# Mixer A of a two-layer hybrid trunk put into a fixed order: projections two heads ahead, both maps' logits side by side, two of mixer B's convolution inputs drawn into A

## The chip, the cores and the metric

The kernel runs on one core of one Trainium2 chip, as one launch. The metric is the device time of an execution in microseconds; the profile of one execution is read beside it.

## What is computed

512 tokens of width 1024 go through two layers. The even layer normalizes, projects once into mixer A (differential attention, 4 heads of 128) and mixer B (an mLSTM, 4 heads, with a causal convolution on q and k), projects the eight heads' results back and adds. The odd layer does so with two other mixers (C and D). After each mixer comes a mixture of 16 experts, then a gated embedding. All is float32. The part that the change is about:

```python
def diff_attention(q, k, v, lam, gain, lam_init):   # 8 maps of width 64, two for each head
    ...
        logits = jnp.einsum('bhqd,bhkd->bhqk', qi, k).astype(jnp.float32) * (d ** -0.5)
        q_chunk = (bi * Q_BLOCK + jnp.arange(Q_BLOCK)) // CHUNK
        logits = jnp.where(key_chunk[None, :] <= q_chunk[:, None], logits, -jnp.inf)
        probs = jax.nn.softmax(logits, axis=-1).reshape(b, nh, 2, Q_BLOCK, s)
        weights = probs[:, :, 0] - lam * probs[:, :, 1]
        return jnp.einsum('bhqk,bhkd->bhqd', weights.astype(v.dtype), v)
    ...
    return rmsnorm(out, gain) * (1.0 - lam_init)
```

Before it q and k are rotated (rope on the two halves of each map's 64 numbers).

## The kernel before

**Weights and projections.** Weights come as one stream of units of [128, 1024], in the order that `_layer_units` lists; a chunk of two units is one DMA on SyncE's queue (line 185). `unit` takes the next one and splits it into two float32r parts: ScalarE casts (line 193), VectorE subtracts (line 194). Four units' parts are held at a time. A product of two such pairs is three float32r products (`mm3`, lines 232 to 234). A unit F gives 128 outputs of all tokens, transposed ([128, 512]; 24 products, `proj_f`); four units T give 512 outputs by token (96 products, `proj_t`), as for V of A, V of B and B's output gate.

**Mixer A.** `rotated` projects q and k of a head, evicts them on ScalarE (line 477), swaps the halves by four DMAs on GpSimd's queue (line 480), multiplies the swapped copy by the sines on GpSimd (line 481) and rotates on VectorE (lines 482 and 483). It is written one head ahead. For each of four tiles of 128 queries, `logits` makes for each of the two maps a product of 64 rows (map 0 lies on partitions 0 to 63, map 1 on 64 to 127; line 499), adds the mask by a bfloat16 product on all 128 rows (line 500), and calls `softmax_block`: maximum (line 360), its negative (361), exponential with sum (362), reciprocal (363). Map 0's mask and softmax come before map 1's product. Lines 511 to 513 combine the two maps, `put_T` transposes (369) and copies (370) the combined weights, `pv` multiplies by the values (383). `mean_ln` squares the result (333), splits the squares (334, 335), sums them by products with ones (338, 339) and takes the logarithm (341); lines 517, 518 and `finish` (406, 407) scale the head and split it for the output projection.

**Order.** The engines' instructions are placed by a planner that reorders freely, from its own estimates of cost; program order counts only through data, the rooms of tiles and the order of the weight units. So V and the gate of B, written after A, run among A's heads. One part of the kernel, the gated embedding, stands in a region `tc.manual_schedule(engines=MS)`, in which TensorE, VectorE and ScalarE keep the order that is written. GpSimd and the DMA queues stay with the planner there.

**PSUM.** Four banks "m" (projections) and four banks "w" (the rest) are taken in turn.

**Mixer B.** After V and gate of B, `convolved(n)` projects q and k of a head and runs convolution and silu from PSUM, one head ahead of the head's own products. The output projection of A's four heads (`out_proj(mix)`, two halves of the width) is written ahead of B's last head, that of B's heads after it.

Of the kernel before, what the change touches and what calls it, by code (L numbers as in the profile page):

```python
# [8 lines left out]
F32 = mybir.dt.float32  # L9
F32R = mybir.dt.float32r  # L10
# [6 lines left out]
S = 512  # L17
# [11 lines left out]
# columns of the constants that follow from the shapes  # L29
# [4 lines left out]
# columns of the small parameters  # L34
# [17 lines left out]
# rooms that the units of a further block take in turn  # L52
# [14 lines left out]
def _layer_units(layer):  # L67
    """Order in which the units of [128, 1024] weights are used."""
    if layer == 0:
# [3 lines left out]
        u += [("T", 5, k) for k in range(4)] + [("T", 6, k) for k in range(4)]  # L73
        for n in range(NH):
            u += [("F", 3, n), ("F", 4, n)]
# [30 lines left out]
def tile_hybrid_trunk(ctx, tc, x, wst, gains, small, lam, rwt, cst, out, stop=None):  # L106
# [72 lines left out]
    def load(src, eng=None, pool=None, c=None):  # L179
        """A chunk of two units."""  # L180
# [7 lines left out]
    def split(src, a=None, place=None):  # L188
        """Two parts of a unit."""
# [9 lines left out]
    def ahead(eng=None, pool=None):  # L199
        """Load the next chunk of the stream before its units are asked for."""  # L200
# [35 lines left out]
    def norm_scale(t, xn, r):  # L236
        """1 / sqrt(mean(h^2) + eps) of a tile's tokens; xn is room for the squares."""
# [42 lines left out]
    def values(v):  # L280
        """Values by token, [128, tile, 128] for each head."""
# [19 lines left out]
    def rows_split(r, rows):  # L301
        """Rows of four heads as two exact parts, on partitions 0 and 32."""
# [9 lines left out]
    def log_sigmoid_rows(r4, ps, r0, bias):  # L312
        """log(sigmoid(rows + bias)) at partitions 0 to 3, and a spare row."""
# [9 lines left out]
    def cols_of(c, rows):  # L323
        """Rows [4, 512] as columns [128, tile, head]."""
# [5 lines left out]
    def mean_ln(tmp, src, scale):  # L330
        """log(scale * sum over partitions of src^2 + eps), on every partition."""
# [12 lines left out]
    def out_proj(mix):  # L344
        m = len(mix)
        for nh in range(2):
# [64 lines left out]
    banks(ctx, m=4, w=4)  # L411

    def even_mixer():
        with ExitStack() as cx:
# [31 lines left out]
            # gates of the mLSTM  # L446
# [17 lines left out]
            # rows of the results that no block may write  # L464
# [6 lines left out]
            # A  # L471
# [931 lines left out]
```

## Time and profile before

| | |
|---|---|
| time of the runs | 1485.28, 1489.43, 1491.0 us; median 1489.43 |
| span of the profiled execution | 1487.2 us (no other time is given for that execution) |
| busy share of the span | TensorE 94%, VectorE 75%, ScalarE 62%, GpSimd 9% |
| instructions | 18591 |
| mean granted clock of TensorE | 0.974 |

The span runs from the first to the last instruction of the profiled execution. The busy time of TensorE counts each matmul to its modelled end, so that two in a row overlap on paper; how fast it works is read from the starts. Granted clock 1.00 is 2.4 GHz, 0.50 is 1.2 GHz. A wait is put down to the instruction that ended it.

### The profile page before, as it was taken

Reading aid. Unit: us, or ns where it says so; the run is one execution under the profiler, and the core shown is the slowest. Engines: PE = TensorE matmul, PEld = TensorE weight load, DVE = VectorE, ACT = ScalarE, POOL = GpSimd, SP = SyncE. Lnnn points to the kernel's source line nnn. Section 1 sums busy time; section 2 is a strip of 40 time slices with the busy share of each in tenths; the row PEclk is TensorE's granted clock in tenths of the full one; section 3 lists DMA queues with packets and bytes.
Section 4 is the critical chain, followed back from the end, with each engine's and each line's share of the span. In section 5 each row is a group of like instructions: output and inputs, shape, how many; then the busy total and the mean of one; then the engine's idle time right before and its main releaser. Section 6 shows DMA issues by size and latency. Waiting matters only on the chain. (4 is left out here: it accounts for less than half of the span.)

```text
span 1487.2 us, 18591 instructions
## 1 busy us (share of the span) xinstructions
PE 1396.7 (94%) x6728; PEld 1096.0 (74%) x6728; DVE 1118.5 (75%) x1633; ACT 916.9 (62%) x1424; POOL 136.9 (9%) x143
## 2 busy tenths in 40 slices
PE   6999999969987999999999999999969989999996
PEld 4765677748865888877787887878648868888875
DVE  5466568679976999987776556575589979999875
ACT  4334566348865888885655536452448868888855
POOL 2121012010000000003011000100010000000030
PEclk9998999989999999999999999999989999999998
DMA  9331123478985999915431111111478989999261
GB/s 346 134 95 43 57 85 119 186 265 322 412 353 210 410 404 410 396 74 221 142 113 37 50 57 58 58 49 37 198 265 325 420 338 404 404 407 387 93 252 57
DMA packets 54652, 323.28 MB, mean 217 GB/s; under 512 B 6481, under 2 KB 6897, under 8 KB 23569
## 3 DMA queue, kind: packets, MB, share of 16 engines
q1 hardware_dynamic: 36576, 250.38, 43.7%
q0 software_dynamic: 12640, 52.16, 9.4%
q10 hardware_dynamic: 5328, 19.40, 3.3%
q8 instruction: 57, 0.93, 0.3%
q14 instruction: 51, 0.41, 0.1%
HBM read 292.55 MB, written 27.26 MB: 215 GB/s over the span
## 5 line engine op out<-in xcount | busy, mean ns | idle before, releaser
L194 DVE TENSOR_TENSOR wlo<-raw,whi 128x1024 fp32r<-128x1024 f32 x478 | 565.8, 1223 | 92.6 <-ACT whi L193 91.1
L193 ACT CAST whi<-raw 128x1024 fp32r<-128x1024 f32 x478 | 492.3, 1055 | 166.3 <-PE m L234 94.8
L232 PE MATMUL m<-whi,eh 128*128 128x512 f32 x528 | 213.4, 404 | 1.6 <-ACT whi L193 1.6
L233 PE MATMUL m<-wlo,eh 128*128 128x512 f32 x528 | 210.6, 399 | 1.5 <-DVE wlo L194 1.4
L234 PE MATMUL m<-whi,el 128*128 128x512 f32 x528 | 210.0, 398 | 0.0
L233 PE MATMUL m<-xtl,whi 128*128 128x512 f32 (+1 forms) x368 | 142.5, 388 | 0.8 <-DVE xtl L257 0.8
L234 PE MATMUL m<-xth,wlo 128*128 128x512 f32 (+1 forms) x368 | 142.9, 389 | 0.0
L232 PE MATMUL m<-xth,whi 128*128 128x512 f32 (+1 forms) x368 | 141.7, 386 | 0.5 <-ACT xth L256 0.5
L232 PE MATMUL m<-whi,xth 128*128 128x512 f32 x288 | 118.3, 412 | 2.7 <-ACT xth L256 1.2
L233 PEld LDWEIGHTS m<-wlo,eh 128*128 128x128 f32 x528 | 100.3, 190 | 25.6 <-DVE wlo L194 3.4
L232 PEld LDWEIGHTS m<-whi,eh 128*128 128x128 f32 x528 | 100.4, 190 | 25.1 <-ACT whi L193 2.1
L234 PE MATMUL m<-whi,xtl 128*128 128x512 f32 x288 | 117.1, 408 | 1.6 <-DVE xtl L194 1.1
L234 PEld LDWEIGHTS m<-whi,el 128*128 128x128 f32 x528 | 99.9, 189 | 24.3 <-DVE el L842 0.8
L233 PE MATMUL m<-wlo,xth 128*128 128x512 f32 x288 | 116.8, 406 | 0.5 <-DVE wlo L194 0.5
L232 PE MATMUL m<-whi,hh 128*128 128x512 f32 x256 | 102.9, 407 | 0.0
L233 PE MATMUL m<-wlo,hh 128*128 128x512 f32 x256 | 101.8, 399 | 0.3 <-DVE wlo L194 0.3
L234 PE MATMUL m<-whi,hl 128*128 128x512 f32 x256 | 102.0, 399 | 0.0
L233 PEld LDWEIGHTS m<-xtl,whi 128*128 128x128 f32 x368 | 70.6, 192 | 13.0 <-DVE xtl L257 1.0
L232 PEld LDWEIGHTS m<-xth,whi 128*128 128x128 f32 x368 | 70.5, 192 | 12.7 <-ACT xth L256 0.9
L234 PEld LDWEIGHTS m<-xth,wlo 128*128 128x128 f32 x368 | 70.5, 192 | 11.7 <-issue 0.7
L849 POOL DMA_INDIRECT xg<-xrow,toki x32 | 34.1, 1066 | 488.6 <-PE w L839 432.9
L841 ACT CAST eh<-w 128x512 fp32r<-128x512 f32 x82 | 46.9, 590 | 39.1 <-PE w L839 37.8
(427 smaller groups left out, 2307.0 us busy)
## 6 DMA issues: line engine op xcount, KB each, us to landing
raw<-in_wst_dram SPq DMA_DIRECT2D x226, 1024.0 KB, 7.8
raw<-in_wst_dram POOLq DMA_DIRECT2D x14, 1024.0 KB, 7.5
yrow<-y ACTq DMA_DIRECT2D x17, 512.0 KB, 8.6
yrow<-gbc ACTq DMA_DIRECT2D x14, 512.0 KB, 8.3
xrow<-raw POOLq DMA_DIRECT2D x8, 512.0 KB, 6.3
yrow<-tmp POOLq DMA_DIRECT2D x14, 256.0 KB, 9.8
h<-in_x_dram SPq DMA_DIRECT2D x4, 512.0 KB, 13.1
sw<-qk POOLq DMA_DIRECT2D x16, 128.0 KB, 2.8
```

The source lines that it names most:

```text
L193: nc.scalar.copy(hi, src)
L194: nc.vector.tensor_sub(lo, src, hi.bitcast(F32))
L232: mm(ps, l[0], r[0], start=start, stop=False)
L233: mm(ps, l[0], r[1], start=False, stop=False)
L234: mm(ps, l[1], r[0], start=False, stop=stop)
L841: W.turned = nc.scalar.copy(eh[o], ps)
L849: ins = nc.gpsimd.indirect_dma_start(out=xg, out_offset=None, in_=xrow, in_offset=bass.IndirectOffsetOnAxis(ap=idx, axis=0))
```

## The change

- The stream of weights has the eight units of V and gate of B after the F units of B's heads 0 and 1, instead of ahead of them.
- Mixer A becomes a region of fixed order on TensorE, VectorE and ScalarE. Heads count on: "heads" 4 and 5 are q and k of B's heads 0 and 1, projected and evicted in A without rotation. While head n runs, the projection of n + 2 is written in pieces between its steps.
- Of a tile, both maps' products come first, then both masks; the maxima come out negated; one reciprocal serves both maps; for tiles 2 and 3 the scaling of map 1 moves from VectorE to ScalarE.
- The multiplication by the sines moves from GpSimd to VectorE.
- A head's ending is written in two parts: squares and their split at its end (`result`), the rest (`normed`) after the next head's first exponentials.
- Pairs 2 and 3 of q and k lie in the room of B's gate `og`.
- In B, `convolved(0)` and `convolved(1)` read SBUF; heads 0 and 1 project for 2 and 3; the two halves of A's output projection stand beside B's heads 2 and 3.
- `softmax_block` (used by mixer D) takes the negated maximum directly.

Comments and docstrings fall away too. The diff without these:

```diff
@@ _layer_units
-        u += [("T", 5, k) for k in range(4)] + [("T", 6, k) for k in range(4)]
         for n in range(NH):
+            if n == 2:
+                u += [("T", 5, k) for k in range(4)] + [("T", 6, k) for k in range(4)]
             u += [("F", 3, n), ("F", 4, n)]
@@ out_proj
-    def out_proj(mix):
+    def out_proj(mix, *halves):
         m = len(mix)
-        for nh in range(2):
+        for nh in halves or range(2):
@@ softmax_block
-        nc.vector.reduce_max(nm[:, 0:1], ps[:, :n], axis=AX.X)
-        ts(nm[:, 1:2], nm[:, 0:1], -1.0, None, op0=OP.mult)
+        nc.vector.reduce_max(nm[:, 1:2], ps[:, :n], axis=AX.X, negate=True)
@@ even_mixer, A (the lines that it takes out are 473 to 519 above)
             mix = []
+            order = ExitStack()
+            order.enter_context(tc.manual_schedule(engines=MS))
+            og = mp.tile([128, T, 512], F32, name="og", bufs=1)
+            pairs = [mp.tile([128, 2, S], F32, name="qk") for _ in range(2)]
+            pairs += [og[:, 2 * i:2 * i + 2, :] for i in range(2)]
+            pairs += [mp.tile([128, 2, S], F32, name="qk") for _ in range(2)]
+            units, banks_, lg, pr, sw = {}, {}, {}, {}, {}
+            def take(n, j):
+                units[n, j] = unit("F", 8)
+            def project(n, j, k0=0, k1=KD):
+                if k0 == 0:
+                    banks_[n, j] = pm([128, S])
+                w = units[n, j]
+                for k in range(k0, k1):
+                    mm3(banks_[n, j], (w[0][:, k, :], w[1][:, k, :]), (xt[0][:, k, :], xt[1][:, k, :]), k == 0, k == KD - 1)
+            def evict(n, j):
+                act(pairs[n][:, j, :], banks_[n, j], AF.Copy, scale=0.125 if n < NH and j == 0 else 1.0)
+            def swap(n):
+                if n < NH:
+                    sw[n] = mp.tile([128, 2, S], F32, name="sw", bufs=1)
+                    for q in range(4):
+                        nc.gpsimd.dma_start(out=sw[n][q * 32:(q + 1) * 32], in_=pairs[n][(q ^ 1) * 32:(q ^ 1) * 32 + 32])
+            def rotate(n):
+                if n < NH:
+                    tt(pairs[n], pairs[n], cosb, op=OP.mult)
+                    tt(sw[n], sw[n], sinb, op=OP.mult)
+                    tt(pairs[n], pairs[n], sw[n], op=OP.add)
+            def logits(n, i):
+                if n == NH:
+                    return
+                nk, qk = 128 * (i + 1), pairs[n]
+                lg[i] = [pw([128, S]) for _ in range(2)]
+                for m in range(2):
+                    r = slice(64 * m, 64 * m + 64)
+                    mm(lg[i][m][:, :nk], qk[r, 0, i * 128:(i + 1) * 128], qk[r, 1, :nk], start=True, stop=False)
+                for m in range(2):
+                    mm(lg[i][m][:, nk - 128:nk], identb, maskc, start=False, stop=True)
+            def exps(i):
+                nk = 128 * (i + 1)
+                nm = st.tile([128, 3, 2], F32, name="nma", bufs=4)
+                p = [tmp() for _ in range(2)]
+                for m in range(2):
+                    nc.vector.reduce_max(nm[:, 0, m:m + 1], lg[i][m][:, :nk], axis=AX.X, negate=True)
+                for m in range(2):
+                    act(p[m][:, :nk], lg[i][m][:, :nk], AF.Exp, bias=nm[:, 0, m:m + 1], accum_out=nm[:, 1, m:m + 1])
+                pr[i] = p, nm
+            def combine(i):
+                nk = 128 * (i + 1)
+                p, nm = pr[i]
+                nc.vector.reciprocal(nm[:, 2, :], nm[:, 1, :])
+                tt(nm[:, 1, 1:2], nm[:, 2, 1:2], nlam, op=OP.mult)
+                if i < 2:
+                    ts(p[1][:, :nk], p[1][:, :nk], nm[:, 1, 1:2], None, op0=OP.mult)
+                else:
+                    act(p[1][:, :nk], p[1][:, :nk], AF.Copy, scale=nm[:, 1, 1:2])
+                stt(p[0][:, :nk], p[0][:, :nk], nm[:, 2, 0:1], p[1][:, :nk], op0=OP.mult, op1=OP.add)
+            def turn(wt, i):
+                ps = pm([128, 4, 128])
+                for j in range(i + 1):
+                    nc.tensor.transpose(ps[:, j, :], pr[i][0][0][:, j * 128:(j + 1) * 128], ident)
+                nc.scalar.copy(wt[:, :i + 1, i * 128:(i + 1) * 128], ps[:, :i + 1, :])
+            def result(n, wt):
+                o = pw([128, S]) if n == NH - 1 else pm([128, S])
+                for j in range(T):
+                    mm(o[:, j * 128:], va[n][:, j, :HD], wt[:, j, j * 128:], start=(j == 0), stop=(j == T - 1))
+                sq, hi, lo = tmp(), tmp(F32R), tmp(F32R)
+                act(sq, o, AF.Square)
+                nc.scalar.copy(hi, sq)
+                tt(lo, sq, hi.bitcast(F32), op=OP.subtract)
+                return o, hi, lo
+            def normed(n, o, hi, lo):
+                ps = pw([128, S]) if n == NH - 1 else pm([128, S])
+                one = oner.to_broadcast([128, 128])
+                mm(ps, one, hi, start=True, stop=False)
+                mm(ps, one, lo, start=False, stop=True)
+                l = tmp()
+                act(l, ps, AF.Ln, bias=epsc, scale=1.0 / HD)
                 act(l, l, AF.Exp, scale=-0.5)
                 stt(l, o, sgain, l, op0=OP.mult, op1=OP.mult)
                 mix.append(finish(xp, l))
+            take(0, 0)
+            take(0, 1)
+            project(0, 0)
+            evict(0, 0)
+            take(1, 0)
+            project(0, 1)
+            evict(0, 1)
+            swap(0)
+            take(1, 1)
+            project(1, 0)
+            evict(1, 0)
+            project(1, 1)
+            rotate(0)
+            evict(1, 1)
+            swap(1)
+            take(2, 0)
+            logits(0, 0)
+            logits(0, 1)
+            done = None
+            for n in range(NH):
+                a = n + 2
+                wt = mp.tile([128, 4, S], F32, name="wt", bufs=1)
+                exps(0)
+                project(a, 0, 0, 2)
+                if done:
+                    normed(*done)
+                project(a, 0, 2, 5)
+                combine(0)
+                exps(1)
+                rotate(n + 1)
+                turn(wt, 0)
+                logits(n, 2)
+                project(a, 0, 5)
+                take(a, 1)
+                combine(1)
+                exps(2)
+                evict(a, 0)
+                turn(wt, 1)
+                logits(n, 3)
+                project(a, 1, 0, 3)
+                combine(2)
+                exps(3)
+                turn(wt, 2)
+                project(a, 1, 3)
+                combine(3)
+                evict(a, 1)
+                swap(a)
+                if n + 1 < NH:
+                    take(a + 1, 0)
+                turn(wt, 3)
+                logits(n + 1, 0)
+                logits(n + 1, 1)
+                done = n, *result(n, wt)
+            normed(*done)
+            order.close()
@@ even_mixer, B
             def convolved(n):
-                qk = mp.tile([128, 2, S], F32, name="qk")
-                q, k = qk[:, 0, :], qk[:, 1, :]
-                conv_silu(tmp, proj_f(unit("F", 8)), P_CB + 4 * n, q)
-                conv_silu(tmp, proj_f(unit("F", 8)), P_CB + 4 * (NH + n), k, HD ** -0.5)
+                if n < 2:
+                    q, k = [pairs[NH + n][:, j, :] for j in range(2)]
+                    src = q, k
+                else:
+                    qk = mp.tile([128, 2, S], F32, name="qk")
+                    q, k = qk[:, 0, :], qk[:, 1, :]
+                    src = [proj_f(unit("F", 8)) for _ in range(2)]
+                conv_silu(tmp, src[0], P_CB + 4 * n, q)
+                conv_silu(tmp, src[1], P_CB + 4 * (NH + n), k, HD ** -0.5)
                 return q, k
-            nxt = convolved(0)
+            todo = [convolved(0), convolved(1)]
             for n in range(NH):
-                q, k = nxt
-                if n + 1 < NH:
-                    nxt = convolved(n + 1)
-                if n == NH - 1:
-                    out_proj(mix)
+                q, k = todo.pop(0)
+                if n < 2:
+                    todo.append(convolved(n + 2))
+                else:
+                    out_proj(mix, n - 2)
```

## Rows read from the trace of the kernel before

**Rows 1.** Stretches of the even mixer: from 104 us, where mixer A's heads run among V and the gate of B, and from 190 us, mixer B's heads and both output projections. Columns: start:end length, then for PE, PEld, DVE, ACT and POOL the busy us and the number of instructions, the granted TensorE clock, the DMA share and GB/s.

```profile
104.00:190.00 86.00, 83.97 (x324) 53.02 (x323) 51.45 (x131) 42.11 (x107) 8.00 (x8) 0.94 0.17 57
190.00:307.00 117.00, 116.40 (x533) 90.89 (x532) 80.34 (x144) 59.30 (x129) 14.90 (x14) 1.00 0.40 149
```

**Rows 2.** Who waited for whom, TensorE alone, from 55 to 310 us: the two rows of mixer A. Columns: us in total, times, longest us.

```profile
PE w L339 <- DVE tmp L335: 1.9, 2, 1.6
...
PE w L369 <- DVE nm L363: 0.5, 1, 0.5
```

**Rows 3.** The stretch of lower granted clock within mixer A, columns as in rows 1.

```profile
113.80:124.00 10.20, 10.20 (x23) 6.28 (x24) 5.95 (x21) 3.65 (x11) 0.00 (x0) 0.50 0.00 0
```

**Rows 4.** Time line around the longest wait in A: start us, length us, engine, line, operation, out<-in, shapes, count, and in brackets the idle time before and what ended it.

```profile
109.69 3.41 POOL L481 TENSOR_TENSOR sw<-sw,ce 128x1024 f32<-128x1024 f32 x1 [1.35 <-DMA sw<-qk]
...
110.79 2.85 DVE L335 TENSOR_TENSOR tmp<-tmp 128x512 fp32r<-128x512 f32 x1
...
113.69 0.76 PE L339 MATMUL w<-tmp,oner 128*128 128x512 f32 x1 [1.56 <-DVE tmp L335]
...
114.25 0.63 PE L232 MATMUL m<-whi,xth 128*128 128x512 f32 x1
...
114.68 0.63 PE L233 MATMUL m<-wlo,xth 128*128 128x512 f32 x1
```

**Rows 5.** Time line of TensorE at the last tile's logits of head 0 (both maps, each a pair of instructions and a mask) and at the projection products behind them.

```profile
94.71 1.12 PE L499 MATMUL w<-qk 64*128 64x512 f32 x2
95.76 0.23 PE L500 MATMUL w<-maskc,identb 128*128 128x128 bf16 x1
95.92 1.12 PE L499 MATMUL w<-qk 64*128 64x512 f32 x2
96.98 0.23 PE L500 MATMUL w<-maskc,identb 128*128 128x128 bf16 x1
97.02 0.48 PE L233 MATMUL m<-xtl,whi 128*128 128x512 f32 x1
97.33 0.39 PE L234 MATMUL m<-xth,wlo 128*128 128x512 f32 x1
97.56 0.39 PE L232 MATMUL m<-xth,whi 128*128 128x512 f32 x1
```

**Rows 6.** Time line of the ending of one head in A, after its value product: squares, their two parts, logarithm and exponential of the mean, the scaling and the high part of the result.

```profile
162.29 0.60 ACT L333 ACTIVATE tmp<-w 128x512 f32<-128x512 f32 x1 [2.51 <-PE w L383]
...
162.92 0.62 ACT L334 CAST tmp<-tmp 128x512 fp32r<-128x512 f32 x1
...
163.58 0.69 DVE L335 TENSOR_TENSOR tmp<-tmp 128x512 fp32r<-128x512 f32 x1 [3.65 <-ACT tmp L334]
...
165.55 0.69 ACT L341 ACTIVATE tmp<-w,epsc 128x512 f32<-128x512 f32 x1 [2.01 <-PE w L339]
...
166.48 0.62 ACT L517 ACTIVATE tmp<-tmp 128x512 f32<-128x512 f32 x1
...
167.72 0.74 DVE L518 SCALAR_TENSOR_TENSOR tmp<-w,sgain,tmp 128x512 f32<-128x512 f32 x1
...
169.41 0.61 ACT L406 CAST mixh<-tmp 128x512 fp32r<-128x512 f32 x1
```

**Rows 7.** Groups of instructions by line, with shapes kept apart, from 55 to 190 us. Columns: line, engine, operation, out<-in, shapes, count, busy us, mean ns of one, idle us before them.

```profile
L194 DVE TENSOR_TENSOR wlo<-raw,whi 128x1024 fp32r<-128x1024 f32 x15 | 19.6, 1307 | 20.0 <-ACT whi L193 20.0
...
L362 ACT ACTIVATION_READ_ACCUMULATOR tmp<-w,nm 128x1 f32 x32 | 6.3, 196 | 0.0
...
L482 DVE TENSOR_TENSOR qk<-qk,ce 128x1024 f32<-128x1024 f32 x4 | 4.9, 1221 | 3.2 <-DMA sw<-qk 3.2
...
L511 DVE TENSOR_TENSOR c<-nm,lmb 128x1 f32<-128x1 f32 x16 | 3.4, 212 | 0.2
...
L360 DVE TENSOR_REDUCE nm<-w 128x1 f32<-128x256 f32 x8 | 3.3, 419 | 4.1 <-PE w L500 4.1
...
L362 ACT ACTIVATE tmp<-w,nm 128x128 f32<-128x128 f32 x8 | 2.9, 361 | 3.5 <-DVE nm L361 3.5
...
L360 DVE TENSOR_REDUCE nm<-w 128x1 f32<-128x128 f32 x8 | 2.2, 286 | 2.3 <-PE w L500 2.3
...
L513 DVE SCALAR_TENSOR_TENSOR tmp<-tmp,nm 128x256 f32<-128x256 f32 x4 | 1.9, 484 | 0.1
...
L513 DVE SCALAR_TENSOR_TENSOR tmp<-tmp,nm 128x128 f32<-128x128 f32 x4 | 1.4, 349 | 0.0
...
L512 DVE TENSOR_SCALAR tmp<-tmp,c 128x128 f32<-128x128 f32 x4 | 1.1, 278 | 0.1
```

**Rows 8.** The float32 products of the logits (line 499) alone, from 55 to 190 us. Columns: start:end length, PE and PEld busy us and count, granted clock, DMA share, GB/s.

```profile
55.00:190.00 135.00, 26.74 (x64) 9.83 (x64) 0.96 0.22 71
```

**Rows 9.** Two other waits of TensorE, in the odd mixer (time line), each followed by the stretch of lower clock that came after it (columns as in rows 1).

```profile
780.85 0.50 PE L338 MATMUL w<-c,oner 128*128 128x512 f32 x1 [2.23 <-ACT c L334]
...
782.80:786.20 3.40, 3.40 (x10) 2.63 (x9) 1.54 (x3) 3.37 (x7) 0.00 (x0) 0.50 0.00 0
...
1052.47 0.66 PE L375 MATMUL w<-cs,w 128*128 128x128 f32 x2 [1.57 <-DVE nm L361]
...
1052.40:1059.20 6.80, 6.73 (x16) 4.13 (x17) 2.79 (x7) 2.60 (x10) 0.00 (x0) 0.50 1.00 422
```

**Rows 10.** Who waited for whom on SyncE's DMA queue, whole span: the largest row.

```profile
SPq L185 <- DVE wlo L194: 960.7, 199, 33.2
```

More of the change, by code (lines that the diff above doesn't have):

```diff
@@ L472, in even_mixer @@
             mix = []
-            def rotated():
-                qk = mp.tile([128, 2, S], F32, name="qk")
-                for i in range(2):
-                    ps = proj_f(unit("F", 8))
-                    act(qk[:, i, :], ps, AF.Copy, scale=0.125 if i == 0 else 1.0)
-                sw = mp.tile([128, 2, S], F32, name="sw", bufs=1)
-                for q in range(4):
-                    nc.gpsimd.dma_start(out=sw[q * 32:(q + 1) * 32], in_=qk[(q ^ 1) * 32:(q ^ 1) * 32 + 32])
-                nc.gpsimd.tensor_tensor(sw, sw, sinb, op=OP.mult)
-                tt(qk, qk, cosb, op=OP.mult)
-                tt(qk, qk, sw, op=OP.add)
-                return qk
@@ L486, in even_mixer @@
-            qkn = rotated()
-            for n in range(NH):
-                qk = qkn
-                if n + 1 < NH:
-                    qkn = rotated()
-                wt = mp.tile([128, 4, S], F32, name="wt", bufs=1)
-                def logits(i):
-                    nk = 128 * (i + 1)
-                    pr = []
-                    for m in range(2):
-                        ps = pw([128, S])
-                        r = slice(64 * m, 64 * m + 64)
-                        mm(ps[:, :nk], qk[r, 0, i * 128:(i + 1) * 128], qk[r, 1, :nk], start=True, stop=False)
-                        mm(ps[:, nk - 128:nk], identb, maskc, start=False, stop=True)
-                        pr.append(softmax_block(tmp(), ps, nk))
-                    return pr
-                nxt = logits(0)
-                for i in range(T):
-                    nk = 128 * (i + 1)
-                    pr = nxt
-                    if i + 1 < T:
-                        nxt = logits(i + 1)
-                    c1 = st.tile([128, 1], F32, name="c1", bufs=4)
-                    tt(c1, pr[1][1], nlam, op=OP.mult)
-                    ts(pr[1][0][:, :nk], pr[1][0][:, :nk], c1, None, op0=OP.mult)
-                    stt(pr[0][0][:, :nk], pr[0][0][:, :nk], pr[0][1], pr[1][0][:, :nk], op0=OP.mult, op1=OP.add)
-                    put_T(wt, pr[0][0], i)
-                o = pv(va[n], wt)
-                l = mean_ln(tmp, o, 1.0 / HD)
@@ L533, in convolved @@
             def convolved(n):
-                qk = mp.tile([128, 2, S], F32, name="qk")
-                q, k = qk[:, 0, :], qk[:, 1, :]
-                conv_silu(tmp, proj_f(unit("F", 8)), P_CB + 4 * n, q)
-                conv_silu(tmp, proj_f(unit("F", 8)), P_CB + 4 * (NH + n), k, HD ** -0.5)
+                if n < 2:
[7 more added lines that the diff above has]
+                conv_silu(tmp, src[1], P_CB + 4 * (NH + n), k, HD ** -0.5)
                 return q, k
-            nxt = convolved(0)
+            todo = [convolved(0), convolved(1)]
             for n in range(NH):
-                q, k = nxt
-                if n + 1 < NH:
-                    nxt = convolved(n + 1)
-                if n == NH - 1:
-                    out_proj(mix)
+                q, k = todo.pop(0)
[3 more added lines that the diff above has]
+                    out_proj(mix, n - 2)
                 mb = bcast(mrs, n)
```

## The prediction

> **What bounds the kernel now.** I read the page's busy shares first, then the stretches of the even mixer, then TensorE's waits there, then the time line around the worst wait, then the costliest lines by shape. The stretches [rows 1] give TensorE as the bound: 83.97 of 86 us busy from 104 to 190, where mixer A's heads run beside V and the gate of B, and 116.40 of 117 us from 190 to 307. VectorE has a third of the time free, ScalarE half. So a gain has to come out of TensorE's waits, its clock or its own work. The waits of A's lines are small: 1.9 us on the low part of the squares and 0.5 on a transpose [rows 2]. The granted clock is the larger loss: one stretch of 10.2 us at 0.50, the lower level [rows 3], where float32r products start 0.43 us apart [rows 4] against 0.23 at full clock [rows 5]; half of it, 5.1 us, is lost. What TensorE did before it: 1.56 us of idleness, since a subtraction of 512 columns took 2.85 us on VectorE beside a 3.41 us multiplication on GpSimd [rows 4]; alone the same form takes 0.69 [rows 6].
>
> **The change, part by part.** The sum is made against the profiled span of 1487.2 us; the median of the runs is 2.2 us above it, taken as what lies around the span.
>
> Removed: the two waits, -2.4, and the low stretch, -5.1, since the multiplication that held VectorE up moves there as one more operation of 1.22 us [L482 in rows 7]. Whether the new order brings its own is the last term but two.
>
> Logits side by side. Each float32 product is two instructions; a pair with 512 columns runs 1.05 us, then the mask 0.16 when a product on 64 rows follows, 0.04 when a float32r product does [rows 5]. All pairs are 26.74 us busy [rows 8]; less 0.07 for each of 32 modelled ends [rows 5] 24.7 us. No row shows two row halves at once. The bounds are 0, if they take turns as now, and half, -12.4, if they overlap whole. I take a quarter, -6.2: instructions on the same rows take turns 0.53 us apart in these rows, so in the order first, first, second, second only the middle two can share the time. The Trainium skill, "TensorE: Matmul & The Clock Gate", Part 3, says that tiles on different row groups run at the same time, some 4 ns apart; by that the whole half would go, some 8 us of it would come back as longer waits (as below), and the sum would be +6.9 in place of +8.5; no row of this trace shows it. The two masks in a row save about 0.10 a tile (0.16 and 0.04 become some 0.1): 16 tiles, -1.6, between 0 and -3.
>
> The fixed order adds waits; this decides. TensorE, VectorE and ScalarE now take the region's instructions as written. Take a head n of 1 to 3, from the end of the previous head's value product. The chain stands once in [rows 6]: square 0.60, cast 0.62, subtraction 0.69, so 1.97 with hand-overs. The first maxima of the new head stand behind that subtraction on VectorE: two of 0.29, to 2.5. Their exponentials on ScalarE, two of 0.36 and a read of the sum of 0.20 each [rows 7], end at 3.4. Only then come the previous head's logarithm 0.69, exponential 0.62, product 0.74, cast 0.61 [rows 6] and a subtraction like the first, 0.69: to 6.8. And combine(0) stands behind this on VectorE: two small operations at up to 0.21, then 0.28 and 0.35 [rows 7]: 7.8 us. TensorE has 15 projection products at 0.23 [rows 5], 3.5 us, two products of ones and some breaks, 4.4, with 0.4 of waiting for the parts of the squares. It moves on some 0.2 before the modelled end and so comes to the first transpose near 4.6. Wait: about 3.0. Queued behind that transpose are the third tile's logits and the rest of the projection, for which all is ready.
>
> From there the next transpose needs, on VectorE alone, two maxima of 0.42, the next head's rotation of three operations of 1.22, a weight's low part of 1.31, then combine(1), two small operations at up to 0.21, some 0.35 and 0.48 [rows 7]: 7.0 us, less some 0.5 by which operations that follow each other overlap. TensorE fills 4.2: transpose 0.2, four instructions of the third tile's logits at some 0.42 (an estimate from 0.53 at 512 columns) and two masks, 1.8, nine products 2.1. Wait: 2.3 in heads 1 and 2; 0.8 in head 3, which rotates nothing. Later tiles come in time: after tile 1 the two queues have only that tile's work. Head 0 has no previous head to finish; I give it 0.7 at its second transpose and 0.8 before the first projection two ahead, behind the first rotation. In all 3 x 3.4 + 2 x 2.3 + 0.8 + 1.5 = +17.1. Now the V and gate products of B that fill such places today [rows 1] come after A's units in the stream; the rooms for split weights are taken in that order, so those products can fill only the last head's end.
>
> Shorter logits ahead of a wait only lengthen it: the third tile's 0.42 in each of four heads, 1.7, some 0.4 in three heads where the second projection waits for its bank, and 0.5 before the first: 3.4 of the 6.2 come back. Net of the side-by-side order -2.8.
>
> Clock. Idleness of 1.57 and 2.23 us was followed by 6.8 and 3.4 us at 0.50 [rows 9]. So each of three waits of 3.0 us can bring such a stretch. It costs less than half its length, since TensorE would have waited 2.3 us in it: 0 at 3.4 us, about 1.1 at 6.8, 2.8 at 10.2. I take 1.2 each, +3.6, between 0 and 8.4.
>
> Small edits. The swap's four DMAs stay on GpSimd's queue, behind nothing that is new, and have a whole head to land; the multiplication that left that queue only frees it. SyncE's loads come in the new order of units, as many as before. ScalarE takes two scalings of VectorE's per head; it has half its time free [rows 1]. B's first two convolutions read SBUF where they read PSUM; their projections (four units of 24 products at 0.23, 22.4 us) leave B for A, V and gate leave A for B, TensorE's work is equal. Half an output projection beside head 2 and half beside head 3 leave 48 products, 11 us, of filler for each. TensorE is covered throughout B now [rows 1], and I cost it at 0; if the last head's chain shows, up to +4. The negated maximum saves one small operation per tile in mixer D, where one wait of 1.57 us stands on it [rows 9]: -0.3, down to -5 if its low stretch goes.
>
> Sum: -2.4 - 5.1 - 1.6 - 2.8 + 17.1 + 3.6 - 0.3 = **+8.5**; 1495.7 of span, **1498 us**. What the mixer loses passes on: the loads wait for rooms that the split frees (960.7 us of SyncE's queue [rows 10]), so nothing later makes it up.
>
> **Rivals.**
> 1. The waits do not form, because the planner sets B's products among the region's or the chain runs ahead, and the row halves overlap whole: -2.4 - 5.1 - 1.6 - 12.4 - 0.3 + some 3 = -18.8, 1471 us; with a quarter of overlap 1477. For it: TensorE almost never waits today with the same operations. Against: the written order puts the previous head's ending ahead of combine(0). It decides where less than about 12 us of the 20.7 of waits and clock stand.
> 2. About half of the waits are filled and the clock holds: 8.6 - 2.4 - 5.1 - 1.6 - 2.8 - 0.3 = -3.6, 1486 us; no measurable change.
> 3. Every wait is followed by 10.2 us at 0.50 and the halves take turns: 17.1 + 8.4 - 9.4 = +16.1, 1506 us; two more stretches behind the 2.3 us waits at 5.1 each make it 1516.
> 4. The row halves do not overlap at all, so that this part of the change does nothing: +2.8 on the sum, 1501 us.
>
> **How the numbers follow.** The forecast's case, with rival 4 inside, has half the chance; its own range is 1491 to 1504, and three fifths of it lie above the bound. About 0.5%, 7.4 us, is what a measurement of this kernel can tell from no change. Rival 3 has 0.15, rival 1 0.25 (0.22 of it faster than 1482), rival 2 0.10. Slower 0.30 + 0.15 = 0.45; same 0.20 + 0.10 + 0.03 = 0.33; faster 0.22. The range 1474 to 1512 leaves out the far half of rival 1 and rival 3's extra stretches.
>
> **What would show it.** In the changed profile TensorE's waits in A should stand on the combined weights (line of combine) at the first transpose, some 3 us, and at the second, some 2 us, in heads 1 to 3, each first one followed by a granted clock of 0.50. No multiplication by the sines on GpSimd, no subtraction of squares above 1 us. The second map's first product should start with the first map's second. I am wrong if TensorE is busy through the region as it is now, if V of B's products lie among A's heads, or if the clock stays at 1.00 over waits of 3 us.

## The result, and the profile after

Over seven runs of each kernel the median went from 1489.43 to 1497.97 us (1495.69 to 1502.11): a ratio of 1.0078, 95% interval 1.0057 to 1.0098. Three executions, of 2281.67 us (third experiment), 2299.94 us (last experiment) and 3490.54 us (the kernel before, beside the first four experiments), took half as long again as the others or more, and are left out of every median and ratio below. The profiled execution after took 1498.15 us with a span of 1496.4, 9.2 above the one of before. The loss is made in the even mixer: its end, taken where TensorE's wait within the router's transposes ends, moves from 309.86 to 320.81 us, by 10.95.

Windows of the kernel after, columns as in [rows 1]; they answer to those rows.

```profile
104.00:190.00 86.00, 71.26 (x290) 46.59 (x289) 47.32 (x92) 44.90 (x100) 2.05 (x5) 0.90 0.15 56
190.00:313.00 123.00, 122.57 (x560) 95.79 (x559) 78.34 (x141) 60.37 (x137) 15.20 (x12) 1.00 0.39 146
```

Among A's heads TensorE is idle for 14.7 of 86 us, before it was 2.0; in B it is as busy as before. Who waited for whom, TensorE from 55 to 313 us (answers to [rows 2]):

```profile
PE m L544 <- DVE tmp L539: 17.4, 7, 3.1
PE m L562 <- DVE tmp L555: 0.7, 3, 0.2
```

Line 539 is combine's last operation, line 544 the transposition behind it. The time line of head 1, from the previous head's squares to the first transposition, is the chain of [rows 6] again, and combine(0) behind it:

```profile
101.11 0.60 ACT L553 ACTIVATE tmp<-m 128x512 f32<-128x512 f32 x1 [2.51 <-PE m L551]
...
102.40 0.69 DVE L555 TENSOR_TENSOR tmp<-tmp 128x512 fp32r<-128x512 f32 x1 [3.02 <-ACT tmp L554]
...
103.00 0.48 DVE L525 TENSOR_REDUCE nma<-w 128x1 f32<-128x128 f32 x2
...
104.03 0.69 ACT L564 ACTIVATE tmp<-m,epsc 128x512 f32<-128x512 f32 x1
...
105.41 0.75 DVE L566 SCALAR_TENSOR_TENSOR tmp<-m,sgain,tmp 128x512 f32<-128x512 f32 x1 [1.92 <-ACT tmp L565]
...
106.84 0.69 DVE L407 TENSOR_TENSOR mixl<-tmp,mixh 128x512 fp32r<-128x512 f32 x1 [0.68 <-ACT mixh L406]
...
108.16 0.35 DVE L539 SCALAR_TENSOR_TENSOR tmp<-tmp,nma 128x128 f32<-128x128 f32 x1
...
108.66 0.30 PE L544 MATMUL m<-cs,tmp 128*128 128x128 f32 x1 [2.91 <-DVE tmp L539]
```

The two values that combine(0) needs are there at 104.1; it starts at 107.45, because five operations of the previous head's ending stand before it: logarithm, exponential and cast on ScalarE (lines 564, 565, 406), product and subtraction on VectorE (lines 566, 407). VectorE's part of the time line up to the second transposition shows the rotation and the weight's low part in its way:

```profile
109.09 1.22 DVE L504 TENSOR_TENSOR og<-og,ce 128x1024 f32<-128x1024 f32 x1
110.22 1.22 DVE L505 TENSOR_TENSOR sw<-sw,ce 128x1024 f32<-128x1024 f32 x1
111.48 1.22 DVE L506 TENSOR_TENSOR og<-og,sw 128x1024 f32<-128x1024 f32 x1
112.62 1.22 DVE L195 TENSOR_TENSOR wlo<-raw,whi 128x1024 fp32r<-128x1024 f32 x1
...
114.60 0.48 DVE L539 SCALAR_TENSOR_TENSOR tmp<-tmp,nma 128x256 f32<-128x256 f32 x1
```

Head 3 rotates nothing. But behind the low part that belongs there, at 163.69, come three more, among the second combination's own operations. By the stream's order they split the first three units of B's V, which is written behind the region: the fixed order kept the region's own operations in line, it did not keep these out (VectorE's time line):

```profile
164.90 1.20 DVE L195 TENSOR_TENSOR wlo<-raw,whi 128x1024 fp32r<-128x1024 f32 x1
...
166.03 0.15 DVE L534 TENSOR_TENSOR nma<-nma,lmb 128x1 f32<-128x1 f32 x1
166.09 1.22 DVE L195 TENSOR_TENSOR wlo<-raw,whi 128x1024 fp32r<-128x1024 f32 x1
...
167.23 0.35 DVE L536 TENSOR_SCALAR tmp<-tmp,nma 128x256 f32<-128x256 f32 x1
168.30 1.23 DVE L195 TENSOR_TENSOR wlo<-raw,whi 128x1024 fp32r<-128x1024 f32 x1 [0.72 <-ACT whi L194]
169.44 0.48 DVE L539 SCALAR_TENSOR_TENSOR tmp<-tmp,nma 128x256 f32<-128x256 f32 x1
```

The granted clock fell to 0.50 in or right behind five of these seven waits, those of 2.6 to 3.1 us, and not at the two of 1.5; it was 23.8 us in all against 10.2 before [rows 3]. The two stretches that came with the first waits of heads 1 and 3, of 2.9 us each:

```profile
109.20:112.60 3.40, 3.40 (x11) 1.95 (x8) 3.37 (x3) 1.80 (x6) 0.00 (x0) 0.50 0.00 0
...
160.40:167.20 6.80, 5.89 (x16) 3.64 (x16) 4.87 (x10) 4.01 (x8) 0.00 (x0) 0.50 0.01 2
```

Now the two maps' products, each on its own half of the rows. Time line of TensorE at head 1's last tile (answers to [rows 5]):

```profile
115.57 1.13 PE L516 MATMUL w<-qk 64*128 64x512 f32 x4
...
116.63 0.28 PE L518 MATMUL w<-maskc,identb 128*128 128x128 bf16 x2
```

Four instructions take what two took alone. In the records they start at 115.570, 115.576, 116.103 and 116.110: the first instruction of either map, 6 ns apart, then the second of either, 7 ns apart. All 32 such pairs of the kernel start together, 6 to 14 ns apart. The logits' products alone, from 55 to 190 us (answers to [rows 8]); 6 of these us are at low clock:

```profile
55.00:190.00 135.00, 15.84 (x64) 5.24 (x64) 0.91 0.21 71
```

**Ledger to the mixer's end.** Each TensorE record counts from its start to the next one's, less the idleness between; time at low clock counts half as work and half as loss. The sum runs from TensorE's first product to the mixer's end.

| term, us | before | after | change |
|---|---|---|---|
| idle | 7.3 | 22.8 | +15.4 |
| lost at low clock | 5.1 | 11.1 | +6.0 |
| logits' products, at full clock | 23.5 | 11.7 | -11.8 |
| masks, at full clock | 3.3 | 2.7 | -0.6 |
| transposes, projections and the rest, at full clock | 260.0 | 261.6 | +1.6 |
| sum | 299.3 | 309.8 | +10.6 |

The other 0.4 of the 10.95 lies before TensorE's first product.

### The profile page after: what moved, and what is told of

Read it like the earlier page. It is cut to its first block, busy times and chain, and to the rows that moved or that the text cites. A ratio compares the mean times of both kernels' runs of the same rounds, so it can differ in the third digit from the quotient of the medians.

```text
span 1496.4 us, 18518 instructions
## 1 busy us (share of the span) xinstructions
PE 1391.0 (93%) x6728; PEld 1094.7 (73%) x6728; DVE 1109.1 (74%) x1565; ACT 923.3 (62%) x1436; POOL 128.1 (9%) x139
## 5 line engine op out<-in xcount | busy, mean ns | idle before, releaser
L233 PE MATMUL m<-xth,whi 128*128 128x512 f32 (+1 forms) x368 | 145.9, 397 | 0.6 <-ACT xth L257 0.5
## 6 DMA issues: line engine op xcount, KB each, us to landing
yrow<-tmp POOLq DMA_DIRECT2D x14, 256.0 KB, 10.2
```

Source lines behind the costliest of these rows:

```text
L233: mm(ps, l[0], r[0], start=start, stop=False)
```

## The experiments

Each was timed four to twelve times, beside the kernel before on the same chip; ratios are to that one. The kernel after stands at 1.0078.

**The previous head's ending moved** behind exps(3):

```diff
                 project(a, 0, 0, 2)
-                if done:
-                    normed(*done)
...
                 exps(3)
+                if done:
+                    normed(*done)
```

> The previous head's ending (normed) is written behind the last tile's exponentials instead of ahead of combine(0). Theory (the written order queues that ending on VectorE ahead of the first tile's combination): TensorE's three waits of 2.9 us at the first transpose go, and with them the stretches at 0.50 that followed; the second transpose then waits somewhat longer, since rotation and a split still stand ahead of it. 1489 to 1495 us. Rival (the first transposes wait for something else, or VectorE's whole load of a head sets the pace): the wait reappears in full at the next transpose, 1497 to 1499 us.

Measured: 1500.82 us, 1.0090 [1.0058, 1.0122]. No gain, and a little above the rival's range; the rival holds. The first transposes of heads 1 to 3 wait 0.72 us each instead of 2.9, but the second ones 3.1, 3.1 and 4.5 and the third ones 1.6, 2.7 and 2.8; TensorE from 55 to 325 us:

```profile
PE m L544 <- DVE tmp L539: 23.1, 10, 4.5
```

The ending, moved out of the first transposition's way, now stands in the third one's. The second one's wait has hardly grown in itself: it is 3.0, 3.0 and 4.4 us at full clock in the sixth experiment, and in the kernel after the low stretch ahead of it hid part of that.

**Maps one after the other** in the kernel after (the loop over the masks joined to that over the products):

```diff
                 for m in range(2):
                     mm(... lg[i][m] ... qk[r] ...)
-                for m in range(2):
                     mm(... lg[i][m] ... maskc ...)
```

> Only the side-by-side order is undone: product and mask of map 0, then product and mask of map 1; all else as in the changed kernel. Theory (TensorE waits for the combination, so shorter logits mostly lengthen waits): +3 to +5 us, 1501 to 1503. Rival (the overlap of the row halves is wholly on the path): +11 to +13 us, 1509 to 1511. In the trace the pairs of a tile should run one after the other again, 1.05 us each at 512 columns.

Measured: 1511.40 us, 1.0170 [1.0137, 1.0203]. The rival holds: the overlap is worth 13 us here. The profiled execution (span 1518.0) is the longest of the six, 8 us above their median, so its ledger is read for the parts and not for the total. To the mixer's end its records give +15.0 us on the products (7.1 us more of them at low clock), -3.2 of idleness, and a low clock of 41 us in A in place of 23.8. So the longer products did shorten waits, by a quarter of their own length.

**The side-by-side order alone**, in the kernel before, whose planner still orders the engines:

```diff
+                    ps = [pw([128, S]) for _ in range(2)]
                     for m in range(2):
-                        ps = pw([128, S])
                         ...
-                        mm(ps[:, nk - 128:nk], identb, maskc, ...)
-                        pr.append(softmax_block(tmp(), ps, nk))
-                    return pr
+                    for m in range(2):
+                        mm(ps[m][:, nk - 128:nk], identb, maskc, ...)
+                    return [softmax_block(tmp(), ps[m], nk) for m in range(2)]
```

> The kernel before, with the side-by-side order of the logits alone: both maps' products, then both masks, then both softmaxes; the planner orders the rest as it did. Theory (TensorE is the bound there with hardly a wait, so what the overlap saves of its work comes off the time): -11 to -13 us, 1476 to 1479. Rival (the combination's latency takes it back here too): 1487 to 1490.

Measured: 1484.07 us, 0.9972 [0.9946, 0.9998]; between the two. The mixer ends 5.3 us earlier. Of the 11.8 us only 8.0 (at full clock) are gone, since two maps need two free banks and the planner's order doesn't hold the first map back for the second one's: of 16 tiles 9 overlap whole, 4 in part (the second map starts 0.53 us late, on ScalarE's copy out of a bank, line 370), 3 not at all, with projections set between the maps. TensorE's time line in head 1, one of the second kind and then one of the last:

```profile
125.52 1.65 PE L498 MATMUL w<-qk 64*128 64x512 f32 x4
...
116.55 1.22 PE L498 MATMUL w<-qk 64*128 64x256 f32 x2
117.70 0.29 PE L500 MATMUL w<-maskc,identb 128*128 128x128 bf16 x1
117.75 0.78 PE L234 MATMUL m<-whi,xtl 128*128 128x512 f32 x1
```

Idleness grew by 3.0 and the low clock in A from 10.2 to 13.7 us.

**The planner back** in the kernel after, all else kept:

```diff
-            order.enter_context(tc.manual_schedule(engines=MS))
```

> The changed kernel without the fixed order: the same instructions in the same written order, but the planner may reorder TensorE, VectorE and ScalarE in mixer A. Theory (the waits come from the fixed order): the 18 us of waits shrink below 6 and the stretches at 0.50 fall to two or fewer; 1474 to 1484 us. Rival (the waits come from V and gate of B standing later in the stream, so that there is nothing to fill with): waits stay above 12 us, 1492 to 1500 us.

Measured: 1483.89 us, 0.9984 [0.9964, 1.0003]. The theory holds: this fixed order costs 14 us. The mixer ends at 301.36, 19.5 us earlier than after, with 6.8 us of low clock in A; the profiled execution is the shortest of the twelve, 4 us under their median. Window, and the largest wait from 55 to 190 us, which stands ahead of the first logits, on their rotation:

```profile
104.00:190.00 86.00, 83.48 (x375) 59.36 (x375) 55.77 (x105) 54.69 (x129) 8.38 (x9) 1.00 0.20 68
...
PE w L515 <- DVE qk L505: 3.4, 1, 3.4
```

**Another fixed order.** Is it a fixed order as such, or this one? Of the edit only the lines that it writes are shown:

```diff
+                logits(n, 2)
                 exps(0)
+                logits(n, 3)
+                exps(1); combine(0); combine(1); take(a, 1)
+                if done: normed(*done)
+                exps(2); exps(3)
+                project(a, 0); rotate(n + 1); combine(2)
...
                 logits(n + 1, 1)
+                for i in range(3): turn(wt, i)
+                if n + 1 < NH: take(a + 1, 0)
+                turn(wt, 3)
```

> The kernel after, still with a fixed order in A, but another one: each head begins with its third and fourth tiles' logits, does the previous head's ending behind combine(1), and has all four transposes behind both projections, the rotation of the next head between them. All work is kept. Theory (the waits and the low clock come from where the written order puts the transposes, not from a fixed order as such nor from the load of VectorE or ScalarE): TensorE's 18.6 us of waits in A fall to under 5 and the low stretches in A (23.8 us in the kernel after) to one at most, so 16 to 28 us go: 1470 to 1482 us. Rival (VectorE's and ScalarE's queues set a head's pace whatever the order): the waits come back elsewhere in the head and the time is 1490 to 1500 us.

Measured: 1494.89 us, 1.0042 [1.0022, 1.0062]: by its numbers the rival. The transposes hardly wait any more (0.7 us, once), but others do:

```profile
PE w L516 <- ACT tmp L527: 10.3, 4, 2.8
...
PE m L551 <- ACT wt L545: 4.7, 3, 1.6
```

The third tile's logits, at the head's start, need the banks that exps(0) frees, and exps(0) stands behind the previous head's squares on ScalarE; the value product waits for a copy that I had put behind a weight's high part. The low clock in A is again 23.9 us. So this run doesn't tell order from pace; it has two new faults of the old kind.

**Waits filled with throwaway products**: 72 of 512 columns, whose results the transposes overwrite, set where TensorE waited longest:

```diff
-            def turn(wt, i):
+            def turn(wt, i, fill=0):
                 ps = pm([128, 4, 128])
+                for _ in range(fill):
+                    mm(ps.rearrange(...), xt[0][:, 0, :128], xt[0][:, 0, :], start=True, stop=True)
...
-                turn(wt, 0)
+                turn(wt, 0, 12 if n else 0)
...
-                turn(wt, 1)
+                turn(wt, 1, (13, 6, 6, 11)[n])
```

> The kernel after with 72 throwaway float32r products of 512 columns ahead of the first transposes of heads 1 to 3 (12 each) and the second ones of heads 0 to 3 (13, 6, 6, 11), into the transposes' own bank, which they then overwrite. At 0.23 us each they fill the waits of 2.9, 3.1, 1.5, 1.5 and 2.6 us almost exactly, so that TensorE is late for nothing if the clock holds. Theory (the waits cost their own length and, behind them, half of the low stretches they bring): granted clock 1.00 through A, the 23.8 us at 0.50 gone, 8 to 12 us less: 1486 to 1490 us. Rival (the low stretches cost little, since the next wait takes up what they lose): 1495 to 1500 us, with the clock at 1.00 or not.

Measured: 1501.03 us, 1.0093 [1.0069, 1.0118]; the time is in neither range, nearer to the rival's; in A half of each holds. The clock stayed at 1.00, and 5.2 us of waiting is left at the second transposes, behind the filler:

```profile
104.00:190.00 86.00, 80.00 (x358) 55.43 (x357) 50.89 (x96) 44.32 (x98) 4.03 (x7) 1.00 0.19 68
...
PE m L546 <- DVE tmp L539: 5.2, 3, 1.9
```

The mixer ends at 315.96, 4.85 earlier than after. So of the 11.1 us that the low clock took there, 6.2 were time in which TensorE would have waited for VectorE anyway. The rest of the program then lost those 4.85 and 5 more, with instructions that the edit doesn't touch: some 3 us in the first layer's experts, some 3 in the odd mixer, 4.0 in the wait for the second layer's gathered rows (9.7 us against 5.6). Behind the mixer the clock was at 0.50 for 81.5 us, in the kernel after for 71.6, which makes about half of the loss. Why the clock and that wait came out so is not shown; see the last section.

**B's inputs out of A**: heads 2 and 3 have no projections beside them, B does all eight itself, behind V and the gate:

```diff
-                project(a, 0, 0, 2)
+                if a < NH: project(a, 0, 0, 2)
...   (take, evict, swap and the other parts of project likewise; the units' order to match)
-                if n < 2:
-                    q, k = [pairs[NH + n][:, j, :] for j in range(2)]
```

> The kernel after without the part that draws two inputs of B's convolution into A: heads 2 and 3 have no projections beside them, and all eight projections of B's convolution come in B, behind V and the gate. Theory (the drawn-in products are filler for heads 2 and 3 and nothing else can be, since V and the gate stand behind the fixed order): waits in heads 2 and 3 grow by most of the 22 us that the four projections take, less some 4 us for the splits and evictions that VectorE and ScalarE are spared, B grows by those 22 us: 1510 to 1520 us. Rival (V's or the gate's products are set among heads 2 and 3 instead, as in the kernel before): 1495 to 1500 us.

Measured: 1522.60 us, 1.0235 [1.0206, 1.0264]. The theory holds; the time is a little above its range, and the mixer ends 24.8 us later than after. TensorE's waits from 55 to 190 us, and the window:

```profile
PE m L544 <- DVE tmp L539: 31.0, 11, 5.0
PE m L561 <- ACT tmp L554: 2.7, 2, 1.3
...
104.00:190.00 86.00, 54.80 (x183) 30.82 (x182) 40.79 (x85) 37.50 (x87) 2.04 (x5) 0.68 0.09 31
```

No other product comes in: V and the gate stay behind the fixed order, as in the kernel after, where their first product stands at 179.5 us. What does come in is the splitting of V's first units: three more low parts on VectorE, from 113.62 to 117.43 us, ahead of head 1's second transposition, which waits 4.47 us in place of 1.52.

**The sines on GpSimd again**, as before the change:

```diff
-                    tt(sw[n], sw[n], sinb, op=OP.mult)
+                    nc.gpsimd.tensor_tensor(sw[n], sw[n], sinb, op=OP.mult)
```

> The kernel after with the multiplication by the sines on GpSimd again, as in the kernel before; the order of the other three engines is kept. Theory (VectorE's queue between the first and the second transpose is what the second one waits for): VectorE has 1.2 us less there, the second transposes' waits of heads 0 to 2 (3.1, 1.5, 1.5) fall by about that, head 3's 2.6 stays; with the low stretches 3 to 6 us less: 1492 to 1495 us. Rival (the multiplication on GpSimd takes some 3.4 us and holds up an operation of VectorE beside it, as the 2.85 us subtraction in the kernel before): waits equal or longer, 1498 to 1503 us.

Measured: 1501.13 us, 1.0084 [1.0056, 1.0112]: no gain, as the rival had it, but only in part by its mechanism. In heads 1 and 2 the multiplication takes 2.40 us on GpSimd and holds up nothing on VectorE; VectorE's way from the first to the second combination is shorter by 1.1 us in both, as the theory had it. Head 1's second wait fell from 1.5 to 0.4 us. Head 2's rose from 1.5 to 1.9, because no low stretch came ahead of it here and TensorE was there earlier (at full clock it is 3.0 in the sixth experiment). Head 0's rose from 3.1 to 4.1, where the swapped rows land only at 78.9 and the longer multiplication stands on the chain (time lines of GpSimd and VectorE):

```profile
78.91 3.42 POOL L505 TENSOR_TENSOR sw<-sw,ce 128x1024 f32<-128x1024 f32 x1 [3.66 <-DMA sw<-qk]
...
82.37 1.23 DVE L506 TENSOR_TENSOR qk<-qk,sw 128x1024 f32<-128x1024 f32 x1 [2.27 <-POOL sw L505]
```

To the mixer's end this kernel is 1.9 us ahead of the kernel after, 1.4 of them from before TensorE's first product: in A the gains and the loss cancel. What it has more in the whole lies behind the mixer, with the same code there and 85.6 us of low clock against 71.6.

**The next head's first exponentials early**, a fixed order that mends both faults of the other one (again only the lines that it writes):

```diff
+            exps(0); exps(1)
             done = None
             for n in range(NH):
...
+                combine(0); take(a, 1); combine(1)
+                project(a, 0, 0, 4)
+                if done: normed(*done)
+                logits(n, 2); logits(n, 3); turn(wt, 0); project(a, 0, 4, 6); exps(2)
+                turn(wt, 1); project(a, 0, 6); exps(3); project(a, 1, 0, 3); evict(a, 0)
+                rotate(n + 1); project(a, 1, 3, 5); combine(2); logits(n + 1, 0)
+                project(a, 1, 5); combine(3)
+                if n + 1 < NH: take(a + 1, 0)
+                turn(wt, 2); turn(wt, 3); evict(a, 1); swap(a); logits(n + 1, 1)
+                if n + 1 < NH: exps(0); exps(1)
                 done = n, *result(n, wt)
```

> The kernel after, with another fixed order in A and all work kept: a head's first two maxima and exponentials are written ahead of the previous head's value product and squares, so that combine(0) and combine(1) open the head and the previous head's ending stands behind them; the first two transposes stand inside the first projection, the last two behind both, and the next head's rotation between exps(3) and combine(2). e5 only moved the waits, to the bank that the first maxima free and to the copy behind a weight's split; here both have their work ahead of them. Theory (a fixed order costs what stands ahead of a transposition in VectorE's and ScalarE's queues, nothing else): waits of TensorE in A under 6 us, low stretches in A no more than two, 17 to 25 us less than the kernel after: 1473 to 1481 us. Rival (a fixed order has waits wherever it is cut, since the queues' pace and not the order sets it): waits of 12 us or more, 1488 to 1496 us.

Measured: 1478.72 us (1475.81 to 1480.66), 0.9937 [0.9913, 0.9961]: the theory, and the only kernel here that is clearly faster than before. TensorE's waits from 55 to 190 us, and the window:

```profile
PE m L544 <- DVE tmp L539: 3.2, 3, 2.6
PE w L516 <- DVE nma L533: 1.9, 2, 1.0
...
104.00:190.00 86.00, 80.69 (x358) 58.38 (x357) 56.28 (x95) 54.65 (x121) 9.94 (x9) 0.98 0.24 80
```

The mixer ends at 296.85, 24.0 us earlier than in the kernel after and 13.0 earlier than before; 3.4 us of low clock are left in A. The longest wait, 2.6 us at head 3's last transposition, has the splitting of a unit of V ahead of it: a cast of 1.05 us on ScalarE at 150.51 and a low part of 1.23 us on VectorE at 151.59.

**The same with the maps apart** (the edit of the second experiment):

> The kernel of e9 with the two maps' logits one after the other again (first map and its mask, then second map and its mask), nothing else changed. In e2 the same edit on the kernel after cost 13 us, but there the low clock changed too. Theory (the two row halves run wholly at the same time, and where TensorE has no long waits their worth is the whole half of the products): with waits as in e9 (5 us in A) the time is 11 to 14 us longer: 1489 to 1493 us, and TensorE's products of the logits last 24 to 25 us in place of 12.1. Rival (a part of the overlap was only turned into waits, as the prediction had it, some half): 5 to 8 us longer, 1483 to 1487 us, with A's waits shorter than in e9 by the rest.

Measured: 1487.07 us, 1.0005 [0.9988, 1.0023], 8.4 us more than with the maps side by side by the medians, 10 by the ratios; between the two. The products' row, 55 to 190 us, against 13.14 busy us in the kernel above:

```profile
55.00:190.00 135.00, 25.70 (x64) 9.42 (x64) 0.99 0.24 80
```

From start to start, to the mixer's end, that is +11.5, the masks +1.5, idleness -3.4, the value products -1.5 (the low stretch fell on them in the other kernel). So of the 13.0 us that this order takes off TensorE's work, 3.4 come back as waits even where waits are few.

## Why the prediction came out as it did

The forecast's case happened: the waits stand on the line where it put them, the clock falls with them, and the time is 1497.97 against 1498. The closeness is luck, though: the overlap and the waits were mis-sized in opposite directions. With what the clock cost beyond waiting (4.9) kept apart from the waits at full clock, as the prediction had it:

| term of the sum, us | predicted | measured |
|---|---|---|
| waits removed | -2.4 | -2.4 |
| low stretch removed | -5.1 | -5.1 |
| masks | -1.6 | -0.6 |
| products side by side | -6.2 | -11.8 |
| waits of the fixed order, with what shorter logits add | +20.5 | +23.8 |
| low clock behind them | +3.6 | +4.9 |
| other work of TensorE, by difference to +10.6 | 0 | +1.8 |

The measured waits are the filled kernel's idleness and its 17.5 us of throwaway products, less the 4.9 us of idleness of before that lie outside the two removed waits.

- **The step that failed** is "only the middle two can share the time". I took a float32 product's two instructions to go out before the next product's. The rows show first map, second map 6 or 7 ns later (up to 14 at low clock), and half-way again: each map goes through its own row half without waiting for the other. At full clock that is the whole half, 23.5 to 11.7 us. The Trainium skill, "TensorE: Matmul & The Clock Gate", Part 3, has tiles on different row groups run at the same time; this trace agrees, at 6 to 7 ns between starts.
- **What shorter logits give back.** The sum let 3.4 of 6.2 us come back as waits. The direction was right, the share too large: the second and the last experiment show a quarter (3.2 of 12.3 us of products and masks at full clock, 3.4 of 13.0). So the 3.3 us of waits above the sum are not shown to come from the larger overlap; the next point has 3.6 us of another cause.
- **First transposes of heads 1 to 3**: predicted 3.0 each, measured 2.91, 2.92 and 2.94, on the line named. **Waits for the parts of the squares**: predicted 0.4 in each of these heads, measured 0.22 to 0.23. **Second transposes**: predicted 2.3, 2.3 and 0.8, measured 1.52, 1.45 and 2.56. Low clock before the first two hides part of their lateness: it is 3.0, 3.0 and 4.4 counted with the throwaway products in the filled kernel. Head 3 was the miss, 4.4 against 0.8: no rotation stands before its combine(1), but the three low parts of V's units do, shown with the result, 1.20 to 1.23 us each. The working counted V's products as able to fill only the last head's end and left out the splitting ahead of them. No run takes these three away alone; with the inputs of B out of A they come in head 1, and a wait of 4.47 us with them.
- **Head 0** was given 1.5 at two places; it waited 3.1 at one. Its rotation starts only when the swapped rows have landed, at 80.11, which the working left out.
- **Clock.** "Each first wait followed by 0.50" holds for all three; a second wait in head 3 and head 0's also brought it. The rule used, that a stretch costs less than half its length since a wait follows anyway, is what the filled kernel shows (4.9 of 11.1).
- **Masks** in a row save 0.6, not 1.6. That the square subtraction falls to 0.69 us and that no sine multiplication is on GpSimd are as said. V of B's products appear only at the last head's end; the splitting of its units comes earlier, as said.
- **Mixer D.** Its wait is 1.58 us, before it was 1.57 [rows 9], and now stands on the scaling of the weights (line 891); the low stretch behind it is gone here (44.9 us from 1060.9 to 1105.8, 47.8 before), but back in the kernel of the ninth experiment, with the same code, at 47.9. So that is no effect of the negated maximum.
- **A sum.** 26.74 less 32 times 0.07 is 24.5 us and not 24.7; from start to start the records give 24.65, so nothing hangs on it.
- **Rivals.** The first one named both halves of the best kernel: waits that don't form and a whole overlap. It was priced at 1471 and a reordered kernel reached 1479; what was against it, the ending ahead of combine(0), was a property of this order and not of writing one.

## What to carry to other kernels

When an order is written by hand, walk each engine's queue and ask of every operation on the path what stands ahead of it that nobody needs yet: here the previous head's ending and the next head's rotation stood before a head's first weights, and cost more than the new overlap gave. Moving one such operation only changes which instruction waits; the path has to be cleared through all its hand-overs, free banks and copies among them. Look in the trace, too, for operations from behind the region that were set into its queues: here the splitting of weights that come next. A saving of work on the bound engine counts in full only where that engine isn't waiting.

## What was not expected of the hardware

Two float32 products on two row halves run wholly at the same time: four instructions of 512 columns take 1.13 us, where a pair alone takes 1.12 [rows 5]. A bank that comes free 0.53 us late for the second map cuts the overlap by half.

Behind the mixer all these kernels have the same code, but for mixer D's maximum, yet the time at low clock there lies between 67.8 and 85.6 us, and the odd mixer lasts 322 to 326 us, with its wait on ScalarE [rows 9] at 2.2, 3.4 or 4.6 us. A gain of some 5 us in the first mixer can vanish behind it, as the filled kernel's did. What decides it, none of these runs shows.
